# Pacing a recurrence beside matrix products: no two linked steps in one block

## The chip, the cores and the metric

The kernel runs on one core of one Trainium2 chip. The metric is the device time of one execution in microseconds; the median of several runs counts. TensorE (PE) multiplies matrices, VectorE (DVE), ScalarE (ACT) and GpSimd (POOL) work on elements, and SyncE (SP) issues most of the DMAs. Each engine executes its own instructions in a fixed order and waits on semaphores for the others.

## The reference

One layer of a hybrid encoder: 2048 tokens and 16 learned meta tokens in front, width 1024. An input projection feeds three groups of heads side by side, and their outputs are joined by an output projection; then comes a feed-forward part.

```python
p = rms_norm(h, norm_mix_pre[l]) @ w_in[l]
pa, pb, pc = p[..., :A_COLS], p[..., A_COLS:A_COLS + B_COLS], p[..., A_COLS + B_COLS:]
oa = rg_lru_group(...)               # gated linear recurrence over time, 256 wide
ob = forgetting_attention_group(...) # causal attention with a decay, 8 heads of 64
oc, v_own = rwkv7_group(...)         # matrix-state recurrence, 4 heads of 64:
#   s_kk = S kk_t ;  S = S * w_t - s_kk (kk_t a_t)^T + v_t k_t^T ;  o_t = S r_t
mixed = jnp.concatenate([oa, ob, oc], axis=-1) @ w_out[l]
h = h + rms_norm(mixed, norm_mix_post[l])
f = causal_dwconv(rms_norm(h, norm_ffn_pre[l]) @ ffn_up[l], ffn_conv[l])
gate, val = jnp.split(f, 2, axis=-1)
h = h + rms_norm((gelu(gate) * val) @ ffn_down[l], norm_ffn_post[l])
```

## The kernel before

There are four stages: the input projection with the two recurrences beside it, attention, the output projection, and the feed-forward part. Only the first is touched.

**Products.** The tokens go through the input projection in three parts (`w_in_part`), each of two blocks of tokens (up to 400 wide in part 0, 384 in part 1, 256 in part 2). For each of 24 tiles of 128 output columns and for each of the two blocks, `w_in_step` does 24 matmuls into one PSUM bank `psp`: eight slices of the 1024 inputs, three products each, because every operand is split into a high and a low half (`mm3`, L174 to L176). These 24 matmuls are "a block of products"; a part has 48 of them. The result is copied out by ACT or DVE and stored to scratch memory. `w_in_part` yields after each block, and says whether the tile of columns is complete ("whole"). Ahead of the 48 blocks stands `w_in_gate` with two yields. Between the parts the next tokens are normalised and transposed.

**Recurrences.** Beside the products run the recurrences over the tokens already projected, written as generators that yield after each step. `recurrences` joins them for a part: two gate steps (`gate_block`), and for each of three blocks of up to 256 tokens the RWKV steps p1 (loads, small matmuls L1049 and L1060, reciprocal root), p2 (cumulative sums, L1079, L1100), c1 (scores, L1124) and c2 (transposes L1153, loads for the inversion), then the chain that inverts 16x16 blocks by 15 pairs of a POOL product (L1171) and a DVE sum (L1172), at whose end the generator says `SOLVED`. The ten steps behind that, "the ending", are held back (`R.ending`) and taken when the next block has been brought as far. They are linked, each needing the one before it: A (loads, transpose), B (u1), C (x1 and xf; the x1 sum is L1212), D (u2, matmuls into `rps` from `rwxu` and `rwsc`), D2 (rest of xf), E (L1237), F (L1247), G (state, L1262 to L1282), H (outputs and norm, L1313, L1318), I (L1338, store). B to D2 issue their small matmuls through a helper at L1195. Behind the ending of the block before come the four steps of this block's LRU unit (`lru_block`): for each half of its 256 columns one step with convolution, the two matmuls L1433 and L1434 and the first gates (L1435 to L1441), and one with the square root (L1449), the scan (L1451) and the output (L1460). The two halves share their buffers.

**Pace.** `Beside.advance` is called after each yield of the products. It adds `PACE` = 1.25 to `due` while steps are left, and takes one step for each whole unit of `due`, so every fourth call takes two. The recurrences of a part are added when its 14th tile is whole (the gate counts as the first), that is at the 28th yield. What is left after the last block of part 2 is taken by `finish` without products between.

```python
    def advance(self):
        self.due += self.pace if self.gens else 0.0
        while self.due >= 1.0:
            self.due -= 1.0
            if not self.step():
                break
```

**Order.** The loop's order is not the order of the engines. The kernel is built under a planner (`TileContext(nc, schedule_with_timeline_sim=True)`) that gives each engine its order ahead of the run, by when it reckons an instruction to be ready; among those that are ready the one that was issued first in the loop goes first. So a step's matmuls can stand between those of a later block of products.

Of the kernel before, what the change touches and what calls it, by code (L numbers as in the profile page):

```python
# [303 lines left out]
def w_in_part(core, pools, psum, w_in, blocks, scr, part):  # L304
    yield from w_in_gate(core, pools, psum, w_in, blocks, scr, part)
    units = [("c", 2056 + P * i) for i in range(8)] + [("a", P * i) for i in range(4)]
    units += [(s, c + P * i) for s, c in (("k", 1024), ("v", 1536), ("q", 512)) for i in range(4)]
    waiting = [None]

    def step(*args):  # L310

        after = w_in_step(core, pools, psum, *args, scr)
        if waiting[0]:
            waiting[0]()
        waiting[0] = after

    for kind, c0 in units[:-2]:
        w = w_in_weights(core, pools, w_in, c0, scr, part)
        for block in blocks:
            step(w, block, kind, c0)  # L320
            yield block is blocks[-1]

    last = [(w_in_weights(core, pools, w_in, c0, scr, part), kind, c0) for kind, c0 in units[-2:]]
    for block in blocks:
        for w, kind, c0 in last:
            step(w, block, kind, c0)
            yield kind == "q" and c0 == last[-1][2]
# [118 lines left out]
class Attn:  # L446
# [47 lines left out]
    def next(self, s):  # L494
        self.turn[s] = (self.turn[s] + 1) % len(self.ring[s])
        return self.ring[s][self.turn[s]]
# [319 lines left out]
    def run(self, pool, third):  # L816
# [23 lines left out]
        for i, step in enumerate(ready):  # L840
            if i == len(ready) - 1:
                self.queue = self.nc.gpsimd
            self.weights(*step, lambda share: None)
# [133 lines left out]
class Rwkv:  # L977
# [2 lines left out]

    BLOCKS = 9
    SOLVED = "solved"

    @staticmethod
    def start(b):
# [119 lines left out]
    def chunks(self, b, nch, sg, rav, bk, wc, bon):  # L1105
# [68 lines left out]
        for q in range(parts):  # L1174
            nc.sync.dma_start(dxv[q], ix[q * nblk : (q + 1) * nblk, : 16 * jw])
        yield self.SOLVED

# [6 lines left out]
                xt[16 * q : 16 * q + 16, :, 16 * (q % 2) : 16 * (q % 2) + 16], dx[:ni, q].rearrange("i j s -> j i s")  # L1184
            )
        nc.vector.transpose(xr.rearrange("p i s -> p (i s)"), xt.rearrange("p i s -> p (i s)"))
        yield

        xf = self.t([64, ni, 64], "xf")
        nc.gpsimd.memset(xf[32:64, :, 0:32], 0.0)  # L1190
# [3 lines left out]
        def small(o, lhsT, rhs, lo_out, lo_in):  # L1194
            nc.tensor.matmul(  # L1195
                o[lo_out : lo_out + 32], lhsT[lo_in : lo_in + 32], rhs[lo_in : lo_in + 32], start=True, stop=True,
                tile_position=(lo_in, lo_out),
            )

        for i0, m in groups:  # L1200
# [2 lines left out]
                for q in (0, 32):  # L1203
                    small(ps[:, i], sc[:, i0 + i, 128 + q : 160 + q], xr[:, i0 + i], q, q)
            tt(u1[:, i0 : i0 + m], ps[0:64, :m], m1.to_broadcast([64, m, 32]), op=ALU.mult)
        yield
        for i0, m in groups:
            g = slice(i0, i0 + m)
            ps = self.ps().rearrange("p (i t) -> p i t", t=32)
# [7 lines left out]
            for q in (0, 32):  # L1217
                qs = slice(q, q + 32)
                tt(xf[qs, g, q : q + 32], ps[qs, :m], xt[qs, g], op=ALU.add)
        yield  # L1220
        for i0, m in groups:
            g = slice(i0, i0 + m)
            ps = self.ps().rearrange("p (i t) -> p i t", t=32)
            for i in range(m):
                small(ps[:, i], sc[:, i0 + i, 160:192], x1[:, i0 + i], 32, 0)
            nc.vector.tensor_copy(u2[32:64, g], ps[32:64, :m])
            yield
            ps = self.ps().rearrange("p (i t) -> p i t", t=32)
            for i in range(m):
                small(ps[:, i], u2[:, i0 + i], xf[:, i0 + i, 32:64], 0, 32)  # L1230
            nc.scalar.activation(xf[0:32, g, 32:64], ps[0:32, :m], AF.Copy)
        yield
        for i0 in range(0, ni, 8):
            m = min(8, ni - i0)
            ps = self.ps().rearrange("p (i t) -> p i t", t=64)
# [2 lines left out]
                    ps[0:64, i], sc[64:128, i0 + i, 128:192], w3[64:128, i0 + i, 0:64], start=True, stop=True  # L1238
                )
            nc.scalar.activation(w3[0:64, i0 : i0 + m, 64:128], ps[0:64, :m], AF.Copy)  # L1240
        yield
        ap = self.t([P, 2, ni, 64], "xu")[0:64, 0]
        for i0 in range(0, ni, 4):
            m = min(4, ni - i0)
# [2 lines left out]
                nc.tensor.matmul(ps[0:64, i], xf[:, i0 + i], w3[0:64, i0 + i], start=True, stop=True)  # L1247
            nc.vector.tensor_copy(ap[:, i0 : i0 + m], ps[0:64, :m, 0:64])
            nc.scalar.activation(w3[0:64, i0 : i0 + m, 0:64], ps[0:64, :m, 64:128], AF.Copy)
        yield  # L1250
        gt, rp = self.t([P, m2, CH], "gt"), rav[:, :, 0]
        tt(
            gt[:], k["id2"][:].rearrange("p (o t) -> p o t", o=1).to_broadcast([P, m2, CH]),
# [24 lines left out]
        for c in range(nch):  # L1278
# [5 lines left out]
                        skip_group_check=True,  # L1284
                    )
            nc.vector.tensor_copy(st[:, c + 1], gain[:, c])
        yield

        ntl = -(-nch // 2)
        R_ = min(P, CH * nch)  # L1290
# [38 lines left out]
        rsqrt(nc, r1, ss, t0)  # L1329
        r14 = r1.rearrange("p q (h o) -> p q h o", o=1).to_broadcast([R_, 2 * ntl, 2, 64])  # L1330
        tt(on.rearrange("p q a (h t) -> p (q a) h t", h=2), v4(od), r14, op=ALU.mult)
        yield
        n = CH * nch
        a = CH - META if b == 0 else 0
        for p in range(2):
# [16 lines left out]
        nc.sync.dma_start(  # L1352
            self.scr["mix"][768:1024, t0 : t0 + n - a].rearrange("(p r) t -> r p t", r=P), fo[:, :, a:n]
        )
        yield

# [672 lines left out]


class Beside:


    def __init__(self, pace):
# [5 lines left out]
    def step(self):  # L2042
        while self.gens:
            try:
                next(self.gens[0])
                return True
            except StopIteration:
                self.gens.pop(0)
        return False

    def advance(self):
        self.due += self.pace if self.gens else 0.0
        while self.due >= 1.0:
            self.due -= 1.0
            if not self.step():
                break

    def finish(self):
# [4 lines left out]
def recurrences(core, R, lk, f_bias, scr, blocks, part):  # L2063
# [5 lines left out]
    for b in ((0, 1, 2), (3, 4, 5), (6, 7, 8))[part]:  # L2069
        gen = R.block(b)  # L2070
        while next(gen) != R.SOLVED:
            yield
# [288 lines left out]
```

## Time and profile before

| | |
|---|---|
| median of 3 runs | 3002.75 us (2998.63 to 3002.8) |
| the profiled execution | 3004.56 us, its span 3002.9 us |
| mean granted TensorE clock | 0.973 |
| busy: PE, DVE, ACT, POOL | 97%, 68%, 49%, 44% |
| first and last psp matmul | 41.3 us and 881 us |
| the costliest matmuls of the first stage | three lines x1152, about 380 us each |

The span is the time from the first to the last instruction. A group's row has the line, the engine, the operation, the tiles it writes and reads (`rwxu` is the tile `xu` of the RWKV class, `psp` a bank of products), the shapes, the count, then busy us, mean ns of one, idle us of the engine just before them and which instruction ended that. In the order of time a row begins with its start and duration in us. A matmul's duration overlaps that of the next, so PE's busy share says that there was something in flight, not how fast it went; the granted clock has to be read beside it.

### The profile page before, as it was taken

How to read it: one execution, taken by the hardware profiler on the slowest of the kernel's cores; microseconds unless marked ns; L12 is line 12 of the kernel's file. 1: busy time of each engine (PE TensorE's matmuls, PEld its weight loads, DVE VectorE, ACT ScalarE, POOL GpSimd, SP SyncE). 2: the span in 40 equal slices, each digit the busy share in tenths (PEclk: the TensorE clock that was granted, in tenths of full speed). 3: DMA queues.
4: the chain of work that ended last, by engine and by line, in shares of the span. 5: the costliest groups of instructions: out<-in, count | busy, mean ns of one | idle time of the engine just before them, and what ended most of it. 6: DMA issues, size and time to landing. Idle time of an engine off the chain costs nothing.

```text
span 3002.9 us, 52808 instructions
## 1 busy us (share of the span) xinstructions
PE 2903.4 (97%) x18694; PEld 2493.6 (83%) x18694; DVE 2034.2 (68%) x3937; ACT 1486.1 (49%) x2858; POOL 1322.9 (44%) x1569
## 2 busy tenths in 40 slices
PE   6999999999999999999999999999999999999998
PEld 6998899888886655566568999999999999787887
DVE  5258645665677776565636997898778777656766
ACT  4246332443346554455634666666666665424333
POOL 1002121222224565666843566555654544656443
PEclk9999899999988898999999999999999999999999
DMA  6776469676644347544336566577777764436453
GB/s 213 237 239 219 152 219 316 192 246 193 196 130 94 96 107 208 131 108 112 80 95 213 171 205 183 166 214 214 211 213 215 215 201 129 160 115 221 145 175 120
DMA packets 469191, 530.49 MB, mean 177 GB/s; under 512 B 85711, under 2 KB 355737, under 8 KB 467373
## 3 DMA queue, kind: packets, MB, share of 16 engines
q1 hardware_dynamic: 468156, 526.17, 58.1%
q8 instruction: 147, 2.41, 0.3%
q0 software_dynamic: 768, 0.93, 0.1%
q14 instruction: 120, 0.98, 0.1%
HBM read 368.07 MB, written 158.90 MB: 175 GB/s over the span
## 4 chain that ended last, share of the span: by engine, by line
PE 78%; DVE 8%; DMA 5%; ACT 3%; POOL 3%; issue 2%; SPq 1%; DVEq 0%; POOLq 0%; ACTq 0%
PE psu L174 9%; PE psu L175 9%; PE psu L176 9%; PE psp L174 5%; PE psp L176 5%; PE psp L175 5%; PE po L716 4%; PE psd L174 4%; PE psd L175 4%; PE psd L176 4%; PE mx L566 2%; PE sc L693 2%; PE pswo L174 2%; PE pswo L175 2%; PE pswo L176 2%
## 5 line engine op out<-in xcount | busy, mean ns | idle before, releaser
L174 PE MATMUL psu<-xo,uw 128*128 128x344 f32 x1848 | 586.3, 322 | 6.8 <-ACT ga L1821 3.3
L175 PE MATMUL psu<-xo,uw 128*128 128x344 f32 x1848 | 592.1, 321 | 0.0
L176 PE MATMUL psu<-xo,uw 128*128 128x344 f32 x1848 | 581.7, 320 | 0.9 <-POOL uw L1650 0.9
L174 PE MATMUL psp<-xh,wh 128*128 128x384 f32 (+2 forms) x1152 | 383.0, 332 | 0.0
L176 PE MATMUL psp<-xh,wl 128*128 128x384 f32 (+2 forms) x1152 | 380.1, 330 | 0.0
L175 PE MATMUL psp<-xl,wh 128*128 128x384 f32 (+2 forms) x1152 | 379.6, 330 | 0.0
L174 PEld LDWEIGHTS psu<-xo,uw 128*128 128x128 f32 x1848 | 346.3, 188 | 8.3 <-DVE vb L1841 3.6
L1650 DVE TENSOR_TENSOR uw<-uq,uw 128x512 fp32r<-128x512 f32 x341 | 315.4, 930 | 55.4 <-ACT uw L1649 52.4
L175 PEld LDWEIGHTS psu<-xo,uw 128*128 128x128 f32 x1848 | 347.7, 188 | 0.0
L176 PEld LDWEIGHTS psu<-xo,uw 128*128 128x128 f32 x1848 | 346.2, 188 | 1.1 <-POOL uw L1650 1.1
L1649 ACT ACTIVATE uw<-uq 128x512 fp32r<-128x512 f32 x462 | 288.2, 627 | 107.3 <-PE psu L176 52.7
L571 DVE TENSOR_REDUCE mc<-mx 128x1 f32<-128x512 f32 (+6 forms) x352 | 190.0, 565 | 116.3 <-PE mx L566 82.3
L698 ACT ACTIVATE p<-sc,bias 128x512 f32<-128x512 f32 (+4 forms) x352 | 197.8, 590 | 141.4 <-PE sc L694 119.6
L1789 DVE SCALAR_TENSOR_TENSOR uy<-psu,ffn_cols,uy 128x342 f32<-128x342 f32 (+1 forms) x390 | 220.6, 567 | 69.6 <-ACT uy L1787 67.8
L1797 POOL TENSOR_TENSOR uy<-uy,uy 128x342 f32<-128x342 f32 (+1 forms) x132 | 146.6, 1111 | 229.7 <-ACT uw L1649 69.6
L737 POOL TENSOR_TENSOR acc<-acc,p 128x512 f32<-128x512 f32 (+3 forms) x208 | 222.9, 1073 | 46.2 <-DVE acc L737 21.0
L1650 POOL TENSOR_TENSOR uw<-uq,uw 128x512 fp32r<-128x512 f32 x121 | 179.6, 1484 | 134.4 <-ACT uw L1649 112.9
L174 PEld LDWEIGHTS psp<-xh,wh 128*128 128x128 f32 x1152 | 222.3, 193 | 8.4 <-issue 7.0
L176 PEld LDWEIGHTS psp<-xh,wl 128*128 128x128 f32 x1152 | 222.4, 193 | 7.5 <-issue 5.2
L175 PEld LDWEIGHTS psp<-xl,wh 128*128 128x128 f32 x1152 | 222.5, 193 | 5.0 <-issue 3.2
L1650 DVE TENSOR_TENSOR fo<-u,fo 128x896 fp32r<-128x896 f32 x88 | 101.3, 1151 | 133.1 <-ACT fo L1649 132.6
L1649 ACT ACTIVATE fo<-u 128x896 fp32r<-128x896 f32 x88 | 81.3, 923 | 208.6 <-PE psd L176 113.2
(483 smaller groups left out, 6422.3 us busy)
## 6 DMA issues: line engine op xcount, KB each, us to landing
uq<-scr_us SPq DMA_DIRECT2D x220, 256.0 KB
uq<-in_ffn_up_dram SPq DMA_DIRECT2D x209, 256.0 KB
wl<-scr_wk SPq DMA_DIRECT2D x48, 512.0 KB
wh<-scr_wk SPq DMA_DIRECT2D x48, 512.0 KB
u<-scr_ff SPq DMA_DIRECT2D x88, 256.0 KB
scr_ff<-uy SPq DMA_DIRECT2D x110, 171.0 KB
raw<-in_w_in_dram SPq DMA_DIRECT2D x24, 512.0 KB
scr_wk<-wh SPq DMA_DIRECT2D x24, 512.0 KB
```

The source lines that it names most:

```text
L174: nc.tensor.matmul(out, ah, bh, start=first, stop=False, skip_group_check=more)
L175: nc.tensor.matmul(out, ah, bl, start=False, stop=False, skip_group_check=more)
L176: nc.tensor.matmul(out, al, bh, start=False, stop=last, skip_group_check=more)
L566: nc.tensor.matmul(ps[:rows, : e - a], q3[:, qo : qo + rows], k2[:, a:e], start=True, stop=not last)
L571: self.reduced = nc.vector.tensor_reduce(mc[:rows, i, ci : ci + 1], ps[:rows, : e - a], axis=AX.X, op=ALU.max)
L698: last = nc.scalar.activation(p[:rows, :w], ps[:rows, :w], AF.Exp, bias=bias[:rows, j : j + 1])
L716: mm = nc.tensor.matmul(po[at : at + 64, c0:n], v1[:rows, j], p[:rows, : n - c0], start=start and i < 2, stop=end and i + 2 >= len(group), ...
L737: eng.tensor_tensor(a, ps_[0][0][:rows, c0:n] if start and i == 1 else a, p[:rows, : n - c0], op=ALU.add)
L1649: core.nc.scalar.activation(hi, src, AF.Copy)
L1650: (eng or core.nc.vector).tensor_tensor(lo, src, hi, op=ALU.subtract)
L1789: core.conved = stt(y[:, :n], src[:, i : n + i], cw[:, 44 * i + cc : 44 * i + cc + 1], y[:, :n], op0=ALU.mult, op1=ALU.add)
L1797: core.pooled = nc.gpsimd.tensor_tensor(v[:, :n], g[:, :n], v[:, :n], op=ALU.mult)
```

## The change

A step that ends with a yield inside the ending now yields the mark `FAR` in place of nothing; `recurrences` passes it on, `Beside.step` returns it, and `advance` stops for this call when it has taken such a step. What is owed stays in `due`. A call takes at most `MOST` = 2 steps, so that what is owed is taken at two a call where the steps are unmarked: the LRU steps, the gates, and p1 to c2.

```diff
     BLOCKS = 9
     SOLVED = "solved"
+    FAR = "far"
...
         nc.vector.transpose(xr.rearrange("p i s -> p (i s)"), xt.rearrange("p i s -> p (i s)"))
-        yield
+        yield self.FAR
...
 class Beside:
+    MOST = 2
...
     def step(self):
         while self.gens:
             try:
-                next(self.gens[0])
-                return True
+                return next(self.gens[0]) or True
             except StopIteration:
                 self.gens.pop(0)
         return False

     def advance(self):
         self.due += self.pace if self.gens else 0.0
-        while self.due >= 1.0:
+        for _ in range(self.MOST):
+            if self.due < 1.0:
+                break
             self.due -= 1.0
-            if not self.step():
+            if self.step() in (False, Rwkv.FAR):
                 break
```

The change of `yield` into `yield self.FAR` stands at all ten yields of the ending, behind A, B, C, D, D2, E, F, G, H and I. An unmarked step followed by a marked one can still share a call.

More of the change, by code (lines that the diff above doesn't have):

```diff
@@ L1205, in chunks @@
             tt(u1[:, i0 : i0 + m], ps[0:64, :m], m1.to_broadcast([64, m, 32]), op=ALU.mult)
-        yield
+        yield self.FAR
         for i0, m in groups:
@@ L1219, in chunks @@
                 tt(xf[qs, g, q : q + 32], ps[qs, :m], xt[qs, g], op=ALU.add)
-        yield
+        yield self.FAR
         for i0, m in groups:
@@ L1226, in chunks @@
             nc.vector.tensor_copy(u2[32:64, g], ps[32:64, :m])
-            yield
+            yield self.FAR
             ps = self.ps().rearrange("p (i t) -> p i t", t=32)
@@ L1231, in chunks @@
             nc.scalar.activation(xf[0:32, g, 32:64], ps[0:32, :m], AF.Copy)
-        yield
+        yield self.FAR
         for i0 in range(0, ni, 8):
@@ L1240, in chunks @@
             nc.scalar.activation(w3[0:64, i0 : i0 + m, 64:128], ps[0:64, :m], AF.Copy)
-        yield
+        yield self.FAR
         ap = self.t([P, 2, ni, 64], "xu")[0:64, 0]
@@ L1249, in chunks @@
             nc.scalar.activation(w3[0:64, i0 : i0 + m, 0:64], ps[0:64, :m, 64:128], AF.Copy)
-        yield
+        yield self.FAR
         gt, rp = self.t([P, m2, CH], "gt"), rav[:, :, 0]
@@ L1286, in chunks @@
             nc.vector.tensor_copy(st[:, c + 1], gain[:, c])
-        yield
+        yield self.FAR
         ntl = -(-nch // 2)
@@ L1331, in chunks @@
         tt(on.rearrange("p q a (h t) -> p (q a) h t", h=2), v4(od), r14, op=ALU.mult)
-        yield
+        yield self.FAR
         n = CH * nch
@@ L1354, in chunks @@
         )
-        yield
+        yield self.FAR
 def lru_consts(core, pool, psum, w):
```

## The prediction

> **What bounds the kernel now.** I read the page first, then the first stage in the groups by line, then the count of products at chosen moments, then PE and DVE in order of time around PE's longest waits, then the granted clock around those.
>
> ```profile
> span 3002.9 us, 52808 instructions
> PE 2903.4 (97%) x18694; PEld 2493.6 (83%) x18694; DVE 2034.2 (68%) x3937; ACT 1486.1 (49%) x2858; POOL 1322.9 (44%) x1569
> ```
>
> TensorE is busy for 97% of the span, so what the change is worth is what it does to TensorE's gaps and clock in the first stage. The profiled execution took 3004.56 us, 1.66 us of it outside the span, and stands 1.81 us above the median of 3002.75 us. I add my sum to the median.
>
> From 150 to 890 us, where the recurrences run beside products, PE waits little ahead of the recurrence's matmuls (last columns: busy us, mean ns, idle before, releaser):
>
> ```profile
> L1195 PE MATMUL rps<-rwxu,rwsc 32*32 32x32 f32 x576 | 16.2, 198 | 9.2 <-DVE rwxu L1212 7.5 <-ACT rwsc L1154 1.7
> L1195 PE MATMUL rps<-rwxu 32*32 32x32 f32 x576 | 14.8, 199 | 0.3 <-DVE lru_h L1452 0.3
> L1237 PE MATMUL rps<-rww,rwsc 64*64 64x64 f32 x192 | 15.3, 237 | 0.0
> L1247 PE MATMUL rps<-rww,rwxf 64*64 64x128 f32 x192 | 26.5, 281 | 0.0
> L1282 PE MATMUL rps<-rstate,rwgt 64*64 64x64 f32 x168 | 10.8, 231 | 2.0 <-DVE rwgt L1263 2.0
> ```
>
> One link alone costs PE something: 7.5 us before the D matmuls (L1195 out of rwxu and rwsc), which wait for the x1 sum of step C, L1212 on DVE. The links into E (L1237) and F (L1247) cost 0.0.
>
> **Where the steps really run.** I call 24 psp matmuls a block, of which each part has 48, and count a step's place in blocks. The y-th advance of part p follows 48p + y - 2 blocks, and I counted `due` through both versions by hand. To see where the planner put a step, I take psp alone, from zero to the start of that step's first matmul; the count in brackets divided by 24 is the place (columns: window, its length, PE busy, count, clock, DMA share, GB/s).
>
> ```profile
> 0.00:380.40 380.40, 260.18 (x1392) 0.96 0.66 213
> 0.00:386.30 386.30, 264.94 (x1416) 0.96 0.66 212
> 0.00:393.80 393.80, 271.30 (x1448) 0.97 0.67 213
> 0.00:647.50 647.50, 455.84 (x2424) 0.97 0.70 226
> 0.00:752.80 752.80, 524.72 (x2920) 0.97 0.69 223
> 0.00:838.10 838.10, 580.08 (x3288) 0.97 0.68 219
> ```
>
> Step B of the ending that runs at 393.8 us was issued after block 51 and ran after 1448/24 = 60.3; that at 752.8 us was issued after block 106 and ran after 121.7. The endings run 9 to 16 blocks behind their place, as soon as their own chain lets them, with products filled in between. The two halves of an LRU unit (L1433) are otherwise: those at 380.4, 386.3, 647.5 and 838.1 us ran after 58.0, 59.0, 101.0 and 137.0 blocks, which is where the loop issued them. Place in the program decides when an LRU half runs, and not when a linked step does.
>
> **The change part by part.** Removed: ten advances of the three parts that take two linked steps (B+C, D2+E and so on). The FAR steps move back by up to two blocks. Since they run 9 to 16 blocks late, I cost that at nothing; what hides it is the lag, and were the lag gone, two blocks of delay would cost no PE time while products fill it. The three parts end in the same place: after the last advance both versions have taken everything up to D of the same ending, so the 38 steps behind the products are the same work in the same order. The gate steps and p1, p2, c1, c2 that now go by twos are held by their chain too, and are costed at nothing.
>
> Moved: the LRU units behind each ending. Their four steps go from places 45, 46, 47, 48 to 47, 47, 48, 48 in block 1; 58, 59, 59, 60 to 60, 60, 61, 61 in block 2; 87, 87, 88, 89 to 88, 88, 89, 89 in block 3; 99, 100, 101, 101 to 101, 101, 102, 102 in block 4; 113 to 116 become 115, 115, 116, 116 in block 5; 135, 136, 137, 137 become 137, 137, 138, 138 in block 6. Block 0 and those behind the products stay. A unit issues no POOL work; its SP loads and its one store pass some weight loads, for which PE waits 0.3 us in all, as the waits of the tile psp say (us, times):
>
> ```profile
>   DMA wl<-scr_wk: 0.3, 1
> ```
>
> I take nothing there. What a unit does bring is DVE and ACT work with two activation table loads, and this is what stands in front of L1212 today:
>
> ```profile
> 402.11 0.34 PE L176 MATMUL psp<-xh,wl 128*128 128x384 f32 x1
> 404.65 0.53 PE L1195 MATMUL rps<-rwxu,rwsc 32*32 32x32 f32 x8 [2.21 <-DVE rwxu L1212]
> ```
> ```profile
> 401.35 0.66 DVE L1450 SCALAR_TENSOR_TENSOR rwlg<-rwlg,rwlr 128x256 f32<-128x256 f32 x1 [0.19 <-ACT rwlr L1449]
> 402.04 0.75 DVE L1451 TENSOR_TENSOR_SCAN rwlu<-rwla,lru_h,rwlg 128x256 f32<-128x256 f32 x1
> 402.71 0.25 DVE L1172 TENSOR_REDUCE rwix<-rwitmp 128x8 f32<-128x112 f32 x1
> 402.87 0.28 DVE L1456 TENSOR_SCALAR rwlr<-rwlr 128x256 f32<-128x256 f32 x1
> 403.07 0.15 DVE L1452 COPY lru_h<-rwlu 128x1 f32<-128x1 f32 x1
> 403.19 0.63 DVE L1457 TENSOR_TENSOR rwlr<-rwlr,rwlraw 128x256 f32<-128x256 f32 x1
> 403.74 0.27 DVE L1172 TENSOR_REDUCE rwix<-rwitmp 128x8 f32<-128x120 f32 x1
> 403.93 0.67 DVE L1212 TENSOR_TENSOR rwxu<-rps,rwxu 32x512 f32<-32x512 f32 x1
> ```
> ```profile
> L1449 ACT ACT_TABLE_LOAD x18 | 23.1, 1283 | 0.3
> ```
>
> The LRU half (L1450 to L1457) stands ahead of L1212 in DVE's order, and on the chip it comes late, behind ACT (L1449 loads a table for 1283 ns, once a half). PE's own order has D next, so the products behind D wait too. The other gaps like it:
>
> ```profile
> 562.72 1.19 PE L1195 MATMUL rps<-rwxu,rwsc 32*32 32x32 f32 x32 [0.40 <-DVE rwxu L1212]
> 669.17 1.19 PE L1195 MATMUL rps<-rwxu,rwsc 32*32 32x32 f32 x32 [2.42 <-DVE rwxu L1212]
> 762.91 1.72 PE L1195 MATMUL rps<-rwxu,rwsc 32*32 32x32 f32 x32 [1.80 <-DVE rwxu L1212]
> 850.11 1.13 PE L1049 MATMUL eps<-rwwa,wa_up 64*128 64x256 f32 x4 [0.95 <-ACT rwlg L1437]
> ```
>
> That is one gap for each of LRU units 2 to 6. After four of them the clock was halved for a while (clock is the third figure from the end):
>
> ```profile
> 404.00:412.00 8.00, 7.35 (x50) 7.28 (x51) 3.90 (x9) 0.27 (x1) 0.52 (x1) 0.57 0.17 43
> 671.00:675.00 4.00, 4.00 (x21) 3.64 (x20) 3.49 (x10) 2.11 (x4) 2.12 (x4) 0.57 0.31 102
> 763.00:770.00 7.00, 7.00 (x57) 6.94 (x58) 5.42 (x13) 1.95 (x5) 3.39 (x6) 0.52 0.62 174
> 852.00:856.00 4.00, 4.00 (x31) 3.87 (x30) 3.96 (x9) 3.26 (x7) 1.66 (x3) 0.58 0.23 68
> ```
>
> Lost clock: 8 x 0.43 = 3.4, 4 x 0.43 = 1.7, 7 x 0.48 = 3.4 and 4 x 0.42 = 1.7 us. With its idle time a gap costs 2.21 + 3.4 = 5.6, 0.4, 2.42 + 1.7 = 4.1, 1.80 + 3.4 = 5.2 and 0.95 + 1.7 = 2.7 us: 18.0 us for five, 3.6 on the mean.
>
> The Trainium skill, in "TensorE: Matmul & The Clock Gate", section "Why this matters for your kernels", asks only that PE not idle for over about 3 us between bursts of matmuls. By that rule these gaps would cost their idle time alone; the trace disagrees, with clock 0.57 right behind a wait of 2.21 us.
>
> After the change, the first half of units 2, 4 and 6, which today runs its DVE work ahead of step B, starts one to two blocks later and lands on B to D, and the second half on C to E. Three halves are new on linked steps. Today a half on these steps brought one gap each; I take two of the three, as unit 6 moves least. Sum: 2 x 3.6 = 7.2 us, 3002.75 + 7.2 = 3010.0 us. The ends: no new gap (3002.75), and four new ones at 5.6 each, 22.4 us (3025.2). Units 1, 3 and 5 I take at nothing, between a gap won and a gap more: block 5's unit ran past its place already, and the other two move by one block or into the change of parts.
>
> **Rivals.** *Faster: the gaps before D go.* A single step for each block of products leaves DVE free in time, and the LRU halves come behind C instead of into it. All of L1212's wait (7.5 us) and the clock behind it (3.4 + 1.7 + 3.4 = 8.5) would be 16.0 us, 2986.8 us; with half of the gaps gone, 2994.8 us. For it: a unit two blocks later may miss L1212. Against: pairs are not what makes the gaps. The ending with the gap at 762.91 us had C and D in advances of their own, and the next one, with C and D in one advance, has no gap before D (the four shown make 6.83 of L1212's 7.5 us). I give it 0.28.
>
> *No change.* The planner sets the order by readiness, so the pairs are not in the engines' order to begin with; the change does not do what it says, and the moved halves meet other gaps as often as they leave some. 3002.75 give or take 4 us. For it: the lag of 9 to 16 blocks. Against: the LRU halves do move. 0.21.
>
> *The gaps come, their clock does not.* Two new gaps at their mean idle time, (2.21 + 0.40 + 2.42 + 1.80 + 0.95) / 5 = 1.56 us, make 3.1 us: 3005.9 us, within the bound. This decides where new gaps fall singly and the clock holds through them. Against it stand the four stretches at 0.52 to 0.58. 0.04. The Trainium skill ("TensorE: Matmul & The Clock Gate", "Why this matters for your kernels") would give this time.
>
> **How the numbers follow.** The forecast has 0.47. A measurement of this kernel can tell about 0.2%, 6 us, from no change. Slower by more is the forecast, 0.47; within it the second and third rival, 0.25; faster the first, 0.28. The likeliest case alone spans 3006 (one gap) to 3025. As both signs hold much of the chance, the range reaches from 2990, between half of the gaps and all of them gone, to 3022, short of four dear gaps; about a tenth is left out on each side.
>
> **What would show it.** Right: L1433 of block 2's unit behind x1440 and x1464 psp matmuls (60 and 61 blocks), that of block 4 behind 101 and 102, that of block 6 behind 137 and 138; the B to E matmuls in nearly the same places as now; more idle time before L1195, L1237 or L1247 released by DVE or ACT with L1436 to L1460 in front, and a halved clock behind it. Wrong: idle before L1195 below 4 us and fewer halved stretches between 390 and 870 us (first rival); the same sums within 2 us (second); a different time with the first stage unchanged, the difference then lying where attention begins, where the same recurrence steps run on beside other work and a shifted plan could change waits that I have not costed.

## The result, and the profile after

The changed kernel is slower by 0.29%: 3008.18 us in the median of 22 executions (2996.36 at the least) against 2999.96 us for the kernel before beside it, ratio 1.0029 with a 95% interval of 1.0021 to 1.0036. That is 8.2 us more. The execution profiled took 3011.2 us. Three executions far outside the others, one of the kernel before (3509.11 us) and two of unit 1's kernel below (3682.96 us at a granted clock of 0.701, and 7475.31 us), are left out of the ratios. A ratio, here and below, is not the quotient of the two medians, and lies up to 0.0009 from it.

The page of the changed kernel has the same engines at nearly the same work:

```profile
span 3009.5 us, 52806 instructions
PE 2904.0 (96%) x18694; PEld 2495.1 (83%) x18694; DVE 2040.8 (68%) x3937; ACT 1483.9 (49%) x2858; POOL 1313.6 (44%) x1569
```

TensorE is busy for 0.6 us more, in a span that is 6.6 us longer. Lines behind 983 stand one higher in this kernel: L1212 before is L1213 now, L1195 is L1196 and L1247 is L1248.

The psp products alone, from zero to the start of the first matmul of each half of LRU units 2, 4 and 6 (columns: window, length, PE busy, count, clock, DMA share, GB/s):

```profile
0.00:384.30 384.30, 269.69 (x1440) 0.96 0.67 216
0.00:391.50 391.50, 274.44 (x1464) 0.96 0.68 218
0.00:644.20 644.20, 457.06 (x2424) 0.96 0.70 227
0.00:649.70 649.70, 461.42 (x2455) 0.96 0.70 227
0.00:838.10 838.10, 582.95 (x3288) 0.96 0.68 220
0.00:844.60 844.60, 586.77 (x3314) 0.96 0.68 219
```

Divided by 24 these are 60.0, 61.0, 101.0, 102.3, 137.0 and 138.1 blocks, where before the halves of unit 2 stood at 58 and 59, and one half of units 4 and 6 at 101 and 137.

The waits of PE from 330 us to the last product, grouped (us in total, times, longest), and below them the same gaps in order of time:

```profile
PE rps L1196 <- DVE rwxu L1213: 10.1, 4, 4.1
```
```profile
401.15 0.26 PE L1196 MATMUL rps<-rwxu,rwsc 32*32 32x32 f32 x1 [2.91 <-DVE rwxu L1213]
555.81 0.42 PE L1196 MATMUL rps<-rwxu,rwsc 32*32 32x32 f32 x4 [1.20 <-DVE rwxu L1213]
667.81 0.42 PE L1196 MATMUL rps<-rwxu,rwsc 32*32 32x32 f32 x4 [4.12 <-DVE rwxu L1213]
767.27 0.32 PE L1196 MATMUL rps<-rwxu,rwsc 32*32 32x32 f32 x4 [1.91 <-DVE rwxu L1213]
```

They are the same four gaps before D, of the same units 2 to 5, each longer than it was: 2.91 for 2.21, 1.20 for 0.40, 4.12 for 2.42 and 1.91 for 1.80 us. The fifth, at 850 us before, is gone. Beside each the clock was halved for a while (it is the third figure from the end):

```profile
398.00:406.00 8.00, 5.09 (x44) 0.57 0.28 89
555.00:563.00 8.00, 7.19 (x50) 0.57 0.52 174
665.00:679.00 14.00, 11.19 (x80) 0.51 0.39 132
767.00:775.00 8.00, 7.72 (x61) 0.57 0.74 224
```

By the prediction's own way of pricing, 8 x 0.43, 8 x 0.43, 14 x 0.49 and 8 x 0.43 = 17.2 us of clock, where it was 10.2, and 3.3 us more idle before D less 0.95 at 850 us. That is 9.3 us, as if the forecast were confirmed.

But that way counts only the halvings beside a wait. At 398.8 and 665.0 us the halving began inside the wait, 0.56 and 1.35 us after PE had gone idle. And the clock was halved with no wait at all, in the changed kernel from 863.0 us on, after 3.4 us in which PE was busy throughout, almost wholly with 32x32 matmuls (PE busy and count, clock, DMA share, GB/s):

```profile
859.60:863.00 3.40, 3.40 (x103) 1.00 0.23 81
863.00:866.40 3.40, 3.40 (x17) 0.50 0.02 5
```

The kernel before has three such halvings, of 3.4 us each from 691.6, 773.5 and 858.8 us on, that the prediction did not count. Over all of 330 to 870 us (the kernel before, e1 described below, whose order is that of before, and the changed kernel; the clock is the third figure from the end):

```profile
330.00:870.00 540.00, 528.87 (x4935) 484.22 (x4930) 316.68 (x792) 211.43 (x414) 116.33 (x178) 0.97 0.68 219
330.00:870.00 540.00, 527.49 (x4967) 482.38 (x4963) 319.68 (x800) 212.02 (x416) 116.08 (x178) 0.98 0.69 219
330.00:870.00 540.00, 526.53 (x4822) 480.95 (x4822) 314.25 (x785) 210.57 (x411) 118.21 (x178) 0.96 0.68 218
```

Half of the halvings' length, added up from the traces' clock records, is 15.4, 10.2 and 20.5 us: the two profiles of one order differ by as much as before and after. The stage as a whole does not show the forecast loss either. Two windows, from the first psp product to the last and from there to the first output product (pswo), first before, then after (columns: window, length, busy us and count of PE, PEld, DVE, ACT, POOL, clock, DMA share, GB/s):

```profile
41.50:880.70 839.20, 822.11 (x6808) 758.23 (x6806) 485.72 (x1180) 339.70 (x646) 140.50 (x218) 0.97 0.66 214
880.70:1204.10 323.40, 299.83 (x2315) 194.35 (x2314) 238.50 (x621) 173.93 (x362) 178.07 (x258) 0.87 0.52 130
```
```profile
39.80:877.90 838.10, 820.10 (x6786) 756.70 (x6786) 484.32 (x1175) 339.93 (x644) 140.46 (x219) 0.97 0.66 214
877.90:1210.90 333.00, 302.89 (x2335) 197.95 (x2334) 238.86 (x625) 175.13 (x365) 174.94 (x257) 0.87 0.50 126
```

The first stage is not longer than it was; the stretch behind it, with attention and the last recurrence steps, is 9.6 us longer. Some of this is a boundary: 20 matmuls have changed sides (x6808 to x6786, x2315 to x2335), and PE is busy for 3.06 us more behind it. The rest is idle PE, length less busy: 23.6 us before and 30.1 us now in the stretch behind, 17.1 and 18.0 us in the first stage. What the trace has grown by, then, is mostly waiting of a stage whose program text the change does not move.

The growth lies where the last recurrence steps run beside attention. The last matmuls of their last step (I), before and after:

```profile
1124.49 0.69 PE L1342 MATMUL rps<-rwsg,g_up 128*128 128x64 f32 x2
1131.58 0.52 PE L1343 MATMUL rps<-rwsg,g_up 128*128 128x64 f32 x2
```

They begin 243.8 us after the last product before and 253.7 us after it now; from there to the first output product it is 79.6 and 79.3 us.

### The profile page after: what moved, and what is told of

It is laid out like the page before. It is cut to its first block, busy times and chain, and to the rows that moved or that the text cites. A ratio compares the mean times of both kernels' runs of the same rounds, so it can differ in the third digit from the quotient of the medians.

```text
span 3009.5 us, 52806 instructions
## 1 busy us (share of the span) xinstructions
PE 2904.0 (96%) x18694; PEld 2495.1 (83%) x18694; DVE 2040.8 (68%) x3937; ACT 1483.9 (49%) x2858; POOL 1313.6 (44%) x1569
## 4 chain that ended last, share of the span: by engine, by line
PE 79%; DVE 7%; DMA 5%; ACT 4%; POOL 2%; issue 2%; SPq 1%; DVEq 0%; ACTq 0%; POOLq 0%
PE psu L174 9%; PE psu L175 9%; PE psu L176 9%; PE psp L176 5%; PE psp L175 5%; PE psp L174 5%; PE po L716 4%; PE psd L174 4%; PE psd L175 4%; PE psd L176 4%; PE mx L566 2%; PE sc L693 2%; PE pswo L174 2%; PE pswo L175 2%; PE pswo L176 2%; PE sc L694 2%
## 5 line engine op out<-in xcount | busy, mean ns | idle before, releaser
L1651 DVE TENSOR_TENSOR uw<-uq,uw 128x512 fp32r<-128x512 f32 x341 | 323.6, 954 | 55.9 <-ACT uw L1650 53.0
```

What stands on the lines that cost most here:

```text
L1651: (eng or core.nc.vector).tensor_tensor(lo, src, hi, op=ALU.subtract)
```

## The experiments

Ten of the twelve kernels are the kernel before with `Beside` replaced by a written list: for each block of products, the steps issued behind it, M for the main lane (gates, RWKV steps, endings) and L for a step of an LRU unit. With the list that says what the kernel before does, the engines' orders are those of the kernel before. The last two change one activation instead. In the diffs of the lists the number is the place in blocks.

**Which part of the change costs?** One kernel takes the linked steps and gates as after and the LRU units as before; the other the reverse.

```diff
# e1_links_only (four of the places shown)
-41: "MM"   46: "L"    74: "M"    75: "MM"
+41: "M"    46: "ML"   74: "MM"   75: "M"
...
```

> The linked steps and gates stand at the places of the changed kernel (never two in one block of products), the LRU units at the places of the kernel before. My theory (only the moved LRU units cost anything, the linked steps run 9 to 16 blocks late anyway): ratio 1.000 within 0.0015, and step B to E of every ending behind the same number of psp matmuls as before (x1448 for the ending at 394 us). Rival (spreading the links is itself what costs, by holding the chain back): 1.003.

```diff
# e2_lru_only: units 1 to 6
-45: "ML"  46: "L"  47: "L"   48: "L"
+45: "M"            47: "LL"  48: "LL"
-58: "L"   59: "LL" 60: "L"
+60: "LL"  61: "LL"
-87: "LL"  88: "L"  89: "L"
+88: "LL"  89: "LL"
...
```

> The opposite: the linked steps stand where they did before, in pairs where they were in pairs; the LRU units 1 to 6 go to the places of the changed kernel. My theory: most of the 0.29%, ratio 1.002 to 1.004. Rival (links): 1.000 within 0.0015.

Measured: 0.9999 (0.9987 to 1.0011) for the linked steps alone, 1.0031 (1.0018 to 1.0044) for the LRU units alone. In the first kernel the order of instructions on every engine is that of before, to the last one: with the units at their old places, what the change is named after does nothing. All of the 0.29% comes with the LRU units, which the change moves as a by-product. (With the units moved, the linked steps do count for the order: e2 and the changed kernel, which differ in the steps of the main lane alone, have different orders from block 97 on. It makes no difference that the ratios, 1.0031 and 1.0029, would show.) As its order is that of before, the first kernel also shows what a single profile is worth:

```profile
41.60:876.30 834.70, 815.38 (x6806) 751.29 (x6806) 486.26 (x1179) 339.20 (x646) 140.52 (x218) 0.97 0.67 215
876.30:1197.90 321.60, 298.23 (x2316) 192.98 (x2315) 238.06 (x621) 173.82 (x362) 177.72 (x258) 0.87 0.53 130
```

With the same order, the first stage differs from before's by 4.5 us and the stretch behind by 1.8; the gap before D near 669 us is 3.40 us here and 2.42 us before. The idle PE of that stretch is steadier: 323.40 - 299.83 = 23.6 and 321.60 - 298.23 = 23.4.

**Unit 2, on and off the linked steps.** The prediction took 3.6 us for unit 2's move alone. One kernel makes that move; another puts the unit where no linked step runs near it.

```diff
# e3_unit2_only                       # e8_unit2_clear
-58: "L"   59: "LL"  60: "L"          -58: "L"  59: "LL"  60: "L"
+60: "LL"  61: "LL"                   +67: "L"  68: "L"   69: "L"  70: "L"
```

> Only the LRU unit of block 2 is moved, from places 58, 59, 59, 60 to 60, 60, 61, 61. It comes onto steps B to E of one ending at 390 to 415 us. My sum (one more gap with its halved clock): 3 to 6 us, ratio 1.001 to 1.002, with idle before the D matmul of that ending above today's 2.21 us. Rival (what counts is a shifted plan behind the products, where attention begins, and not the gaps in the first stage): 1.000 within 0.0015, the first stage a few us longer at most and the same order of work from 500 us on.

> Only the LRU unit of block 2 is moved, to 67, 68, 69, 70, behind all linked steps of its ending; the order of work from 500 us on stays that of the kernel before. If LRU work in front of the x1 sum makes the gap before D: the idle time before D near 402 us falls from 2.21 us to under 0.7 us and the halved clock behind it goes, 2 to 6 us faster, ratio 0.998 to 0.9995. If the gap is made by something else on DVE (the inversion's sums, which wait for POOL): the gap stays above 1.5 us, ratio 1.000 within 0.0015.

Measured: 0.9986 (0.9974 to 0.9998) and 0.9989 (0.9975 to 1.0002). Moving unit 2 as the change does makes the kernel 0.14% faster, the fastest of the kernels that only move steps, and faster than both kernels: 2995.95 us against 2998.69 for before. The first was expected slower, with a longer gap; its gap before D near 404 us is 0.69 us, where it was 2.21. In the second the D matmuls of that ending have no wait in front of them (a bracket at the end of the line would name it):

```profile
402.52 1.19 PE L1195 MATMUL rps<-rwxu,rwsc 32*32 32x32 f32 x32
```

So the LRU half in front of the x1 sum was what made the 2.21 us gap; take it away and the gap is gone, and the clock near it stays full (from 395 to 415 us it is 1.00 in both kernels). The second kernel gained 3.5 us in the median from a gap priced at 5.6, and the interval includes none. The gap depends on more than unit 2's place: with unit 1 moved as well (e2 and e10) it is 2.89 and 2.90 us.

**The other units, one at a time.**

```diff
# e4_unit1_only
-45: "ML"  46: "L"  47: "L"   48: "L"
+45: "M"            47: "LL"  48: "LL"
# e7_unit3_only
-87: "LL"  88: "L"  89: "L"
+88: "LL"  89: "LL"
# e6_unit4_only
-99: "L"   100: "L"  102: "M"
+102: "MLL"
# e5_unit6_only
-135: "L"  136: "L"  138: "M"
+138: "MLL"
```

> Only the LRU unit of block 1 is moved, from 45, 46, 47, 48 to 47, 47, 48, 48, to the change of tokens between parts 0 and 1. My sum took nothing for it: 1.000 within 0.0015. Rival (the plan behind it shifts as a whole, down to where attention begins): a ratio off by over 0.0015 in either way, with the difference building up between 880 and 1210 us and not before.

> Only the LRU unit of block 3 is moved, from 87, 87, 88, 89 to 88, 88, 89, 89. My sum took nothing for it: 1.000 within 0.0015. Rival (stretch behind the products): the sign follows the idle time between the last psp and the first pswo matmul, 23.6 us before.

> Only the LRU unit of block 4 is moved, from 99, 100, 101, 101 to 101, 101, 102, 102. My theory as predicted: 3 to 6 us, ratio 1.001 to 1.002, with the gap before the D matmul near 669 us grown from 2.42 us. Rival (stretch behind the products): the sign follows the idle time in that stretch, more than 23.6 us gives slower, less gives faster, whatever the gap at 669 us does.

> Only the LRU unit of block 6 is moved, from 135, 136, 137, 137 to 137, 137, 138, 138. My theory as predicted (a gap in the first stage): 0 to 5 us, ratio 1.000 to 1.0015, found before 880 us. Rival, now likelier (the time is lost between the last psp matmul and the first pswo matmul, 323 us before and 333 us after the change, with PE idle 23.6 us there before and 30.1 after): ratio 1.001 to 1.003, with idle in that stretch at 28 us or more.

Measured: unit 1 1.0003 (0.9982 to 1.0024), which settles nothing, and its profile, of an execution of 3682.96 us, is not read; unit 3 1.0036 (1.0017 to 1.0055); unit 4 1.0013 (0.9997 to 1.003); unit 6 1.0012 (0.9998 to 1.0025). The gap at 669 us, which was to grow with unit 4, is gone there, and the idle time behind the products has grown from 23.6 to 26.0 us; with unit 6 it is 33.2 us, as its rival said. Both intervals include no change. Unit 5, moved alone, changes no engine's order, so it was not run. The whole loss can be had by moving unit 3 by a single block, the unit that the prediction took at nothing. In its profile the first stage is not longer, and PE's waits for the x1 sum in it make 5.1 us, where they made 6.8; what is longer lies behind (the execution profiled took 3005.67 us, 6.2 us less than this kernel's median, so the profile shows only part of the loss):

```profile
39.90:870.90 831.00, 814.60 (x6786) 753.10 (x6785) 484.92 (x1173) 338.95 (x643) 141.80 (x219) 0.97 0.67 216
870.90:1206.90 336.00, 296.79 (x2334) 193.40 (x2334) 239.88 (x627) 173.52 (x365) 172.99 (x257) 0.86 0.50 125
```

That is 39.2 us of idle PE behind the products, against 23.3 on the mean of the four profiles whose order there is that of before (23.6, 23.4, 22.9 and 23.3, for the kernels before, e1, e3 and e8). The same 20 matmuls have changed sides as in the changed kernel. And one wait is 12.9 us long (time, busy, instruction, idle before it):

```profile
1137.85 1.31 PE L566 MATMUL mx<-k,q 128*128 128x400 f32 x3 [12.87 <-DMA k<-scr_cl]
```

It waits for key rows that a DMA brings. The tile that they go into is first cleared by POOL, and POOL had to wait for the last matmul of recurrence step I:

```profile
1125.11 1.83 POOL L491 MEMSET k<- 64x2080 f32 x1 [1.87 <-PE rps L1342]
1132.14 0.23 SPq L530 DMA_DIRECT2D k<-scr_cl  x1
```

So the rows were asked for only at 1132.1 us, 7 us after PE had run out of work (the second line is SP issuing the DMA). In the changed kernel the same wait is 2.0 us, in e2, e5 and e10 it is 1.7, 2.8 and 2.3 us; before, and in the three others with its order there, it is absent.

**All but unit 3.**

```diff
# e10_all_but_unit3: e2_lru_only with unit 3 and unit 5 as before
+87: "LL"  88: "L"  89: "L"
-88: "LL"  89: "LL"
...
```

> Units 1, 2, 4 and 6 at the changed kernel's places, unit 3 (which alone gave 1.0036) as before. If the units' costs simply add: 1.0003 - 0.0014 + 0.0013 + 0.0012 = 1.0014 at most, and the part of the products from 330 to 600 us back to 251 to 256 us from 262. If any shift of the plan costs the stretch behind the products: that stretch at 325 us or more with over 24 us idle, ratio 1.001 to 1.003.

Measured: 1.0009 (0.9999 to 1.0019), with 325.5 us behind the products and 29.0 us of idle PE there, as the second case had it, though its ratio was to be 1.001 or more. Against e2's 1.0031 (1.0018 to 1.0044), leaving unit 3 (with 5) where it was takes back about 0.2%; the two intervals just touch. Unit 3 is the largest part of the loss, but the single costs do not add: 2, 4 and 6 alone come to -0.14 + 0.13 + 0.12 = 0.11%, near this; with unit 3's 0.36 they make 0.47%, above e2's 0.31.

**No unit on linked steps at all.** If the gaps before D were the price, taking units 1 to 5 off them should gain.

```diff
# e9_units_clear
-unit 1: 45 to 48    unit 2: 58 to 60    unit 3: 87 to 89    unit 4: 99 to 101    unit 5: 113 to 116
+unit 1: 52 to 55    unit 2: 67 to 70    unit 3: 94 and 96   unit 4: 110 to 113   unit 5: 128 to 131
```

> The LRU units of blocks 1 to 5 go where no linked step runs, behind the matmuls of G of their ending (52 to 55, 67 to 70, 94 to 96, 110 to 113, 128 to 131); everything else is placed as before. Theory A (LRU work on linked steps costs the first stage, by gaps before D; a shifted plan costs the stretch between the last psp and the first pswo matmul, by PE idle): gaps before D under 4 us in all between 330 and 880 us against 7 to 10, the first stage 3 to 8 us shorter, but the stretch behind it with over 24 us idle and 325 us or more, ratio 0.998 to 1.002. Theory B (only the first stage counts): 0.997 to 0.9985.

Measured: 1.0055 (1.0039 to 1.0072), the slowest of all. The waits from 330 us to 880 us and the two windows:

```profile
PE rps L1195 <- DVE rwxu L1212: 2.6, 3, 1.3
```
```profile
41.20:874.00 832.80, 813.21 (x6774) 751.72 (x6774) 473.57 (x1139) 327.79 (x624) 136.22 (x218) 0.97 0.67 215
874.00:1214.10 340.10, 310.87 (x2347) 198.23 (x2347) 249.32 (x660) 184.64 (x385) 176.25 (x258) 0.85 0.49 125
```

The wait before D fell from 6.8 us to 2.6 and the first stage is 6.4 us shorter than in the profile of before, and yet the kernel is 0.55% slower. Behind the products it has 32 matmuls more, 11.0 us more busy PE (at a clock of 0.85 for 0.87) and 29.2 us of idle PE. Theory B is contradicted. Theory A had the waits, the shorter first stage and the longer stretch behind, but both set the ratio too low (1.002 at most). Nor did the kernel clear the first stage of waits: one of 3.5 us now stands before step C, with LRU work on DVE (L1450, L1451) ahead of the sum of step B (L1205) that C needs:

```profile
760.67 2.54 PE L1195 MATMUL rps<-rwxu 32*32 32x32 f32 x87 [3.52 <-DMA us<-in_ffn_up_dram]
```

The releaser named is a DMA, but L1205 ended at 760.41 us, just ahead of these matmuls. All in all PE is idle for 19.6 us in the first stage, where it was 17.1, and the stage is shorter because PE is busy for 8.9 us less in it, 32 matmuls having left. So the run shows that shorter gaps before D alone do not make the kernel faster, and not what a first stage free of waits would be worth.

**The table loads.** The LRU half comes late on DVE because ACT loads a table for its square root. Replacing the square root by a function of the table already loaded leaves both orders alone and drops 36 of 52 loads: four for each unit, as the table that was there before has to be loaded again. These two kernels leave out the square root, so their LRU output is not the layer's.

```diff
# e11_before_no_table on the kernel before, e12_after_no_table on the changed one
-        nc.scalar.activation(r, r, AF.Sqrt)
+        nc.scalar.activation(r, r, AF.Tanh)
```

> The kernel before with the square root of the LRU units replaced by a tanh, so that ScalarE has no table to load there: 36 loads of 1.283 us fewer, the order on every engine otherwise the same (the LRU's scale is left wrong). If late LRU work behind a table load is what stands in front of the x1 sum: gaps before D fall from 7 us to under 3, and the run is 3 to 10 us shorter, 0.997 to 0.999. If the gap comes from the inversion's chain between POOL and DVE: gaps stay at 5 us or more, 0.999 to 1.000.

> The same in the changed kernel: no square root, no table loads there, order otherwise as in the changed kernel. If the table loads of the moved units are the price of the change, it stands within 0.001 of the run without them on the kernel before. If the price lies in the plan behind the products, the difference of 0.002 to 0.004 between the two stays.

Measured, both against the kernel before: 0.9972 (0.9961 to 0.9984) and 1.0007 (0.9994 to 1.002). The loads cost something in either kernel, 9.6 us before by the medians. But the changed kernel remains 0.35% behind (1.0007/0.9972 = 1.0035), and the intervals do not touch. D's group, which also holds B's matmuls (last columns: idle before, releaser), first without loads on the order of before, then on that of after:

```profile
L1195 PE MATMUL rps<-rwxu,rwsc 32*32 32x32 f32 x576 | 15.8, 197 | 6.0 <-DVE rwxu L1212 4.9 <-ACT rwsc L1154 1.2
```
```profile
L1196 PE MATMUL rps<-rwxu,rwsc 32*32 32x32 f32 x576 | 18.0, 204 | 8.2 <-DVE rwxu L1213 7.4 <-ACT rwsc L1155 0.8
```

From 7.5 to 4.9 us, and from 10.1 to 7.4: the loads make some 2.6 us of the wait in both kernels, so they are not what the change costs. The wait that is left, 4.9 us, lies between the two cases named (under 3, and 5 or more): the loads are one part of it.

All of it in one table (us; first stage and stretch behind as above, of one profile each; idle is the length of the stretch less PE's busy time; the last column is the time from the last product to the last two matmuls of step I, L1342):

| kernel | ratio | first stage | stretch behind | idle PE in it | matmuls in it | last step I |
|---|---|---|---|---|---|---|
| before | 1 | 839.2 | 323.4 | 23.6 | 2315 | 243.8 |
| e1, linked steps | 0.9999 | 834.7 | 321.6 | 23.4 | 2316 | 241.5 |
| e3, unit 2 | 0.9986 | 831.3 | 322.3 | 22.9 | 2315 | 243.7 |
| e8, unit 2 clear | 0.9989 | 836.4 | 324.2 | 23.3 | 2315 | 246.2 |
| e10, all but 3 | 1.0009 | 835.1 | 325.5 | 29.0 | 2315 | 247.3 |
| e5, unit 6 | 1.0012 | 834.7 | 332.0 | 33.2 | 2314 | 250.8 |
| e6, unit 4 | 1.0013 | 827.5 | 324.3 | 26.0 | 2309 | 247.1 |
| after | 1.0029 | 838.1 | 333.0 | 30.1 | 2335 | 253.7 |
| e2, all units | 1.0031 | 835.7 | 325.9 | 30.5 | 2315 | 247.4 |
| e7, unit 3 | 1.0036 | 831.0 | 336.0 | 39.2 | 2334 | 253.6 |
| e9, units clear | 1.0055 | 832.8 | 340.1 | 29.2 | 2347 | 261.3 |
| e11, before, no loads | 0.9972 | 834.9 | 317.3 | 20.2 | 2315 | 237.6 |
| e12, after, no loads | 1.0007 | 832.7 | 328.2 | 33.3 | 2336 | 246.3 |

The ratios do not follow the first stage, whose length already differs by 4.5 us between two profiles of one order (before and e1). They do follow the stretch behind, roughly: with 22.9 to 23.6 us of idle PE in it a kernel takes 0.9986 to 1 of before's time, with 26.0 us and over it takes 1.0009 or more (the kernels without loads aside). They follow the last column as well: up to 246.2 us in the four kernels with before's order there, 247.1 to 261.3 us in the others, 253.6 and more in three of the four slowest. e2 stands out: its profiled execution took 3002.99 us, the lowest of its twelve, and its median is 3010.75, so its row shows least of its loss.

## Why the prediction was right and wrong

**Right: where steps run.** The endings' steps run late, and moving them alone changed nothing, on any engine (e1). The LRU halves run at their place in the program, to the block. That the effect of a change named after the linked steps would lie in the LRU units alone was the reasoning's main step, and e1 and e2 bear it out.

**Right: sign and size.** 7.2 us more were forecast and 8.2 measured, and the range held it. That the sum came so near is luck: neither of the two new gaps that it is made of was found.

**Half right: what makes a gap before D.** The LRU half on DVE in front of the x1 sum does make PE wait (e8 removes one of these gaps with the half). The prediction had two new gaps; there is no new one, and the old ones have grown. Their clock was put down to the gaps, and only in part rightly. Near 402 us the halving went with the gap (e3, e8), but the halvings at 691.6, 773.5 and 858.8 us before have no wait beside them, and make 5.1 us that the prediction's list of lost clock (10.2 us) leaves out. A unit also brings four table loads, not two (36 in nine units).

**Wrong: the term "2 x 3.6 us", gap for gap, in the first stage.** Unit 2, counted at 3.6 us slower, makes the kernel 0.14% faster. Unit 3, counted at nothing because it moves by one block, costs as much as the whole change by itself. Shortening the gaps before D (e9) does not pay. In the changed kernel the first stage took 838.1 us, inside the 831.3 to 839.2 of the four kernels that share before's order behind the products; its idle PE, 18.0 us, is inside theirs too (16.4 to 19.3). If the matmuls that left it are counted back in (3.06 us), it is 841.2 us, 2.0 above the longest of the four: a loss of that size in the first stage cannot be told from the 4.5 us by which two profiles of one order differ, and isn't excluded.

**Wrong: "the 38 steps behind the products are the same work in the same order".** It is true of what the program issues, and not of what the engines run. The planner had filled the last products with steps of an ending, and in the changed kernel it puts 16 matmuls of F and 4 of step p2 (L1080, L1079 before) behind the last product instead of ahead of it. The F group in the stretch behind, before and after:

```profile
L1247 PE MATMUL rps<-rww,rwxf 64*64 64x128 f32 x80 | 12.4, 305 | 0.0
```
```profile
L1248 PE MATMUL rps<-rww,rwxf 64*64 64x128 f32 x96 | 12.6, 274 | 0.0
L1080 PE MATMUL eps<-rwix,spr 4*128 4x256 f32 x4 | 1.1, 400 | 0.0
```

The longest waits of PE there (us, times, longest), before and after, show no single one that took the loss (mx, sc, mc, sh and p are tiles of attention, for its scores, their maxima and their exponentials):

```profile
PE mx L566 <- DVE mc L571: 4.6, 9, 1.9
PE rps L1338 <- DVE rwxu L1331: 3.1, 1, 3.1
PE sc L693 <- ACT p L698: 2.7, 6, 1.0
PE mx L579 <- DVE sh L576: 1.8, 2, 1.0
```
```profile
PE mx L566 <- DVE mc L571: 6.0, 10, 2.4
PE sc L693 <- ACT p L698: 5.9, 9, 2.1
PE mx L579 <- DVE sh L576: 4.4, 3, 2.9
PE rps L1263 <- ACT rww L1250: 2.6, 1, 2.6
PE mx L566 <- DMA k<-scr_cl: 2.0, 1, 2.0
```

Attention's waits for DVE and ACT grew by 1.4, 3.2 and 2.6 us, F's successor G waits 2.6 us for the ACT copy of F's result, and the wait for the key rows is new, while one recurrence wait of 3.1 us went. The prediction named this as the way in which it could be wrong, a difference "lying where attention begins", but gave it no term.

**The rivals.** The first, gaps gone and faster, is contradicted by the waits (10.1 us for 6.8). The second, no change, had its premise right for the linked steps. The third, two new gaps without their clock, did not come either: no gap is new, and beside the old ones the clock was halved. The Trainium skill ("TensorE: Matmul & The Clock Gate", section "Why this matters for your kernels") asks that PE not idle for over about 3 us between bursts of matmuls. Staying below that did not keep the clock here: it was halved from 555.8 us on, right behind a wait of 1.20 us, and from 863.0 us on with no wait.

**Open.** Why the planner's order behind the products comes out worse, when a unit's place changes by a block or two (unit 3's some 320 us earlier), isn't settled. The placements tried change the order down there when unit 1, 3, 4 or 6 moves, and each kernel then waits at other places: 12.9 us for key rows in e7, 3.0 us for POOL's clearing of a key tile in e9, scattered waits in the changed kernel. That PE waits more in these orders, and that the last recurrence step ends later, is measured, in one profile each. That the 20 matmuls behind the last product are the cause is a reading of the table, with e2, e5 and e10 against it. Unit 1's cost is open too.

## What to carry to other kernels

Where a planner sets the order, find from the trace which steps run at their place in the program and which run late behind their own chain: a change of pacing moves only the first kind. Then look beyond the stage: a step moved by one block can alter the plan 320 us later, so compare idle time by stage before pricing the gaps that are in sight. Profile the same order more than once before reading a few us out of a stage's length: here two profiles of one order differed by 4.5 us in the length of the first stage and by 5.2 us in what the halved clock took from it, while the idle time of the stage behind stayed within 1 us in four.

## What the runs showed of the hardware

In the changed kernel the granted clock was halved for 6.8 us beside a PE wait of 1.20 us, and for 13.7 us beside one of 4.12 us. But it was also halved for 3.4 us from 863.0 us on, after 3.4 us in which PE was busy throughout with 32x32 matmuls. Where a wait was removed or cut to 0.69 us (e8, e3, near 402 us), the clock stayed full although the same small matmuls ran. So waits of 1 to 4 us and runs of small matmuls both go with a halved clock here, and these rows do not part their shares. Removing one gap with its halving (e8) gained at most a few us that the measurement can hardly tell from none.

The 36 table loads of 1283 ns on ACT, 46 us in all, cost 9.6 us of 2998.76 (e11), although ACT is busy for only half of the span.
